# Weights fetched two groups ahead instead of three, and loads for row sums issued half an interval sooner

## The chip, the cores and the metric

The kernel is one program on one core of a Trainium2 chip. The metric is device time in microseconds (us) of one execution; lower is better. The engines are named as the profile names them: PE (TensorE, the matrix products), DVE (VectorE), ACT (ScalarE), POOL (GpSimd) and SP (SyncE, which here only issues DMAs). Each engine works through its own instructions in a fixed order, and waits on semaphores for what others write.

## What is computed

One layer of a hybrid encoder: 512 positions, width 2048, one batch entry. Cut to what matters:

```python
mod = jax.nn.silu(c) @ w_cond[layer] + b_cond[layer]
shift, scale, gate = jnp.split(mod, 3, axis=-1)
h = rms_norm(x) * (1.0 + scale[:, None]) + shift[:, None]
proj = h @ w_in[layer]
aq, ak, av, ag, gq, gk, gv, gg, lr_f, lr_b = jnp.split(proj, PROJ_SPLITS, axis=-1)
...  # A) 16 heads of dilated window attention over aq, ak, av, three patterns merged by their softmax sums
a_out = att.reshape(B, S, ATT_WIDTH) * jax.nn.silu(ag)
...  # B) gated linear attention, 4 heads, forward and backward scan, chunks of 64
g_o = rms_norm(o_fwd + o_bwd).reshape(B, S, GLA_WIDTH) * gla_norm_gain[layer]
g_out = g_o * jax.nn.silu(gg)
y = jnp.concatenate([a_out, g_out], axis=-1) @ w_out[layer]
x = x + gate[:, None] * y
return rms_norm(x) * final_gain
```

All is float32. `shift`, `scale` and `gate` depend on `c` alone; so does what `shift` adds to the projections.

## The kernel before, in words

**Stages.** First the condition row and the normalised input are made. Then come the units of the input projection, one after the other on PE: qk2, qk4, qk6 (queries and keys of the attention heads), gk, gv0, gv1 (keys and values of the linear attention), ag0, ag1 (attention gates), gg0, gg1 (linear attention gates), and then the output projection. A unit (`unit`, L1014) computes a block of 512 columns in four PSUM tiles. Its weights come in eight groups of 128x1024 floats. For each group, ACT rounds the raw tile to a high half (`split_hi`, L433, written at L444; for example `gk2h`), DVE subtracts it to get the low half (`split_lo`, L425, written at L430; `gk2l`), and PE makes three products (`three`, L216 to L219): high by high, low by high, high by low.

**Side work.** Between the products of a unit stand other jobs, at positions from 0 to 1 within the unit: attention scores, turns and values in qk2 to gk (`attention`, L712; a score's p at L736, its RECIPROCAL at L740, POOL's scaling at L744, PE's turn into t at L756, and the pieces pt at L760 and L761), the heads of the linear attention in gv1 to gg0 (`gla_head`, L865), and what the change is about, the row sums. In the linear attention, `norm` takes the sum of two squares (gsq, L978 and L981), splits it into gsh (ACT, L988) and gsl (DVE, L989), and PE adds them up over partitions into gn (L990, L991).

**The row sums.** 48 pieces of weights, 128x1024 floats or 512 KB each, are multiplied by a row and summed along the row on DVE: 16 for the bias that `shift` adds (`bias_half`: load L845, sum at L850 for the first half and L316 for the second, tile rawv), and 32 for `gate` (`gate_half`: load L809, sum L316, tile rawg). A name such as v20 or g121 gives the number m and the half z: rawv20 is m = 2, z = 0; rawg121 is m = 12, z = 1. Each has a load and a sum as two jobs of the unit; `some_sums` (L859) gives both their positions, and `SUMS_IN` says how many fall to each unit (4 to qk6, 4 to gk, 9 to gv0, 3 to gv1, 7 to ag0, 8 to ag1, 9 to gg0, the rest to gg1).

**Tiles.** Raw weights and many sum pieces share one pool of four tiles (`RAW`, L247, `bufs=4`). The other sum pieces use two single tiles, "h" and "l": all second halves of the bias, and the odd gate pieces for m below 12 or z = 1. A load waits on SP until its tile is free, and all loads behind it on SP wait with it.

**What sets the order.** PE's order is written out by hand. For DVE, ACT, POOL and SP a scheduler orders the instructions when the program is built, by the order of the code, and jobs of the side list are given some preference (`urgent`, L1008). So when a load moves in the code, its sum can move in DVE's order as well.

**POOL's transfers.** Sums of output weights are formed in DRAM by software DMAs that POOL issues (`paced`, L390; tile T, L393). Each waits until ACT has made a certain high half of a weight.

Of the kernel before, what the change touches and what calls it, by code (L numbers as in the profile page):

```python
# [114 lines left out]
SUMS_IN = {"qk6": 4, "gk": 4, "gv0": 9, "gv1": 3, "ag0": 7, "ag1": 8, "gg0": 9}  # L115
# [63 lines left out]
def block_kernel(ctx: ExitStack, tc: tile.TileContext, a: dict):  # L179
# [21 lines left out]
    def PJ(name):  # L201
        return pp.tile([P, 512], F32, tag="pj", bufs=5, name=name)
# [151 lines left out]
    def fetch(i):  # L354
        if i < len(groups) and i not in raws:
            u, g = groups[i]
            if u == "O":
                raws[i] = out_fetch(g)
            else:
                raws[i] = RAW(f"raw_{u}{g}", [2, 512])  # L360
                nc.sync.dma_start(raws[i], a["w_" + u][g])
# [54 lines left out]
    def block_sums(name):  # L416
        n = SUM_OPS_IN[name]
        r = [sum_ops.pop(0) for _ in range(n)]
        return [((q + 0.5) / n, x) for q, x in enumerate(r)]
# [202 lines left out]
    n = len(chain) // 2  # L622
# [4 lines left out]
    for z in range(2):  # L627
        for e in range(3):
            name = ("mm", "a", 0, 7) if (z, e) == (1, 2) else ("m0", z, e)
# [229 lines left out]
    def some_sums(name):  # L859
        r = [sum_work.pop(0) for _ in range(SUMS_IN.get(name, len(sum_work)))]  # L860
        n = len(r)
        loads = [(max(q - 0.3, 0.1) / n, x[0]) for q, x in enumerate(r)]
        return sorted(loads + [((q + 0.7) / n, x[1]) for q, x in enumerate(r)], key=lambda x: x[0])

    def gla_head(h):  # L865
# [142 lines left out]
    def urgent(go):  # L1008
        with tc.high_priority(offset=20):
            go()  # L1010
# [3 lines left out]
    def unit(name, natural, side=(), lr=None):  # L1014
        side = sorted(spill + list(side) + block_sums(name), key=lambda x: x[0])
        spill[:] = [(at - 1, go) for at, go in side if at >= 1]
        side = [x for x in side if x[0] < 1]
        ps = [PJ(f"ps_{name}_{i}") for i in range(4)]
        pos, tick, ticks = 0, 0, 64
        for g in range(KT // 2):  # L1020
            i0 = gi[name, g]
            split_hi(i0)
            split_hi(i0 + 1)
            for ahead in (2, 3):
                fetch(i0 + ahead)
            split_lo(i0)
            hi, lo = wts[i0]
            for i in range(4):
                for kk in range(2):
                    k = 2 * g + kk  # L1030
                    rh, rl = h_hi[:, k, :], h_lo[:, k, :]
                    if natural:
                        t = slice(i * P, i * P + P)
                        cw = slice(kk * 512, kk * 512 + 512)
                        three(ps[i], rh[:, t], rl[:, t], hi[:, cw], lo[:, cw], k == 0, k == KT - 1)
                    else:
                        c = slice(kk * 512 + i * P, kk * 512 + i * P + P)
                        three(ps[i], hi[:, c], lo[:, c], rh, rl, k == 0, k == KT - 1)
                    tick += 1
                    if tick % 8 == 2:  # L1040
                        split_lo(i0 + 1)
                    while pos < len(side) and side[pos][0] * ticks <= tick:
                        urgent(side[pos][1])
                        pos += 1
                if lr is not None:
                    lr(4 * g + i)
        while pos < len(side):
            urgent(side[pos][1])
            pos += 1
        return ps  # L1050
# [396 lines left out]
```

## Time and profile before

| what | value |
| --- | --- |
| time, median of 3 runs | 948.0 us (945.02 to 949.52) |
| profiled execution | 947.69 us, span 945.9 us |
| mean granted TensorE clock | 0.991 |
| PE busy | 920.1 us, 97% of the span |
| DVE, ACT, POOL busy | 69%, 50%, 10% |
| DVE's waits for rawg loads | 43.8 us in 19 waits |
| SP's waits for a tile of rawg, a gate sum to end (L809) | 41.1 us in 14 waits |
| rawg load, issue to landing, median | 5.3 us |
| POOL's transfer T<-in_w_o, issue to landing, median | 5.2 us |

Rows of a timeline begin with the start and the duration in us; a duration holds the engine's pipeline, so rows of one engine overlap a little at their ends. `[3.49 <-DVE st L736]` at the end says that the engine had been idle for 3.49 us before this row, until DVE wrote st at L736. A list of waits has the total in us, the number, and the longest.

### The profile page before, as it was taken

To read this page: it belongs to the slowest core of one execution; us is meant where nothing else is said; L and a number is where in the kernel's file an instruction comes from. 1 tells how busy PE (TensorE), PEld (TensorE's weight loads), DVE (VectorE), ACT (ScalarE), POOL (GpSimd) and SP (SyncE) were. 2 spreads that over 40 slices of the span, in tenths; PEclk is the share of its full clock that TensorE was granted. 3 is DMA by queue.
4 is the path that set the end of the run, shared out by engine and by line. 5 is a ranking of instruction groups with operands and counts; after the bars stand their busy time and mean duration, and the time that the engine had idled before them with its cause. 6 is when DMAs were issued, how large, how long until landed. Compare 5 with 4: busy or idle time off the path is not lost.

```text
span 945.9 us, 12130 instructions
## 1 busy us (share of the span) xinstructions
PE 920.1 (97%) x4375; PEld 761.9 (81%) x4375; DVE 655.3 (69%) x960; ACT 471.9 (50%) x770; POOL 98.6 (10%) x152
## 2 busy tenths in 40 slices
PE   8999999999999989999999999999999999999996
PEld 6888888888888878788877888878777888888884
DVE  7988899775756666766544656585686629697496
ACT  5553543565655545555413545363553428555464
POOL 0000000022222132122000100111001000000001
PEclk9999999999999989999999999999999999999998
DMA  9999496656656764745766646776766566956753
GB/s 350 404 411 375 183 372 245 223 176 165 191 190 161 220 212 132 236 165 142 212 211 188 185 156 198 223 222 209 248 195 183 184 170 250 324 201 217 276 179 133
DMA packets 54629, 210.84 MB, mean 223 GB/s; under 512 B 7237, under 2 KB 7525, under 8 KB 46249
## 3 DMA queue, kind: packets, MB, share of 16 engines
q1 hardware_dynamic: 48946, 175.89, 51.3%
q0 software_dynamic: 5184, 33.62, 15.0%
q8 instruction: 34, 0.56, 0.2%
q10 hardware_dynamic: 440, 0.57, 0.2%
q14 instruction: 25, 0.20, 0.1%
HBM read 201.57 MB, written 37.84 MB: 253 GB/s over the span
## 4 chain that ended last, share of the span: by engine, by line
PE 78%; DMA 8%; DVE 7%; issue 3%; ACT 2%; POOL 0%; SPq 0%; DVEq 0%; POOLq 0%; ACTq 0%
DMA rawg<-in_wg 5%; PE ps_qk L217 4%; PE ps_qk L218 4%; PE ps_qk L219 4%; PE g L219 4%; PE g L217 4%; PE g L218 4%; PE stb L219 3%; PE ps_gv L219 3%; PE ps_gv L218 3%; PE ps_gv L217 3%; PE stb L218 3%; PE stb L217 3%; PE o L770 3%; PE sta L218 2%
## 5 line engine op out<-in xcount | busy, mean ns | idle before, releaser
L739 ACT ACTIVATE p<-p,st 128x512 f32<-128x512 f32 x64 | 46.1, 720 | 59.7 <-DVE st L736 58.9
L316 DVE CUSTOM_DVE_ANT_0 cb<-cb,sb,c_bcond 128x2048 f32<-128x2048 f32 (+1 forms) x32 | 73.5, 2295 | 0.8 <-DMA cb<-in_wm 0.8
L393 POOL DMA_DIRECT2D T<-in_w_o x48 | 33.5, 705 | 317.7 <-ACT qk21h L444 119.8
L744 POOL TENSOR_SCALAR p<-p,st 128x512 f32<-128x512 f32 x62 | 45.0, 726 | 201.3 <-DVE st L740 153.1
L761 DVE TENSOR_TENSOR pt<-t,pt 128x512 fp32r<-128x512 f32 x64 | 43.8, 688 | 16.3 <-ACT pt L760 16.0
L736 DVE CUSTOM_DVE_ANT_0 p<-s,g 128x512 f32<-128x512 f32 x64 | 43.7, 687 | 14.2 <-PE s L733 14.0
L756 PE MATMUL t<-c_ident,p 128*128 128x128 f32 x256 | 39.1, 275 | 5.2 <-DVE st L736 3.5
L756 PEld LDWEIGHTS t<-c_ident,p 128*128 128x128 f32 x256 | 31.5, 141 | 15.6 <-issue 4.2
L760 ACT ACTIVATE pt<-t 128x512 fp32r<-128x512 f32 x64 | 37.9, 591 | 10.6 <-PE t L756 9.5
L770 PEld LDWEIGHTS o<-pt,vv 128*128 128x128 f32 x256 | 35.5, 193 | 3.0
L770 PE MATMUL o<-pt,vv 128*128 128x256 f32 x256 | 36.2, 285 | 0.0
L316 DVE CUSTOM_DVE_ANT_0 rawg<-rawg,crow,gate 128x1024 f32<-128x1024 f32 x16 | 20.4, 1282 | 22.5 <-DMA rawg<-in_wg 22.5
L316 DVE CUSTOM_DVE_ANT_0 rawg<-rawg,crow,c_bcond 128x1024 f32<-128x1024 f32 x16 | 20.4, 1282 | 21.2 <-DMA rawg<-in_wg 21.2
L740 DVE RECIPROCAL st<-st 128x1 f32<-128x1 f32 x64 | 10.3, 161 | 23.7 <-ACT p L739 23.7
L732 PE MATMUL s<-ks,qs 128*128 128x512 f32 x64 | 25.1, 392 | 0.0
L733 PE MATMUL s<-kl,qs 128*128 128x512 f32 x64 | 25.0, 390 | 0.0
L944 ACT ACTIVATE sq<-st,sc 128x256 f32<-128x256 f32 x24 | 12.2, 506 | 21.2 <-DVE st L934 13.4
L850 DVE CUSTOM_DVE_ANT_0 rawv<-rawv,shb 128x1024 f32<-128x1024 f32 x8 | 10.0, 1250 | 16.4 <-DMA rawv<-in_wv 16.4
L777 DVE TENSOR_TENSOR cat<-o,oh 64x256 f32<-64x256 f32 x32 | 13.3, 415 | 11.0 <-ACT oh L773 10.7
L773 ACT ACTIVATE oh<-o 64x256 f32<-64x256 f32 x32 | 12.2, 382 | 16.9 <-PE o L770 16.0
L1272 POOL TENSOR_SCALAR x<-x,rn 128x512 f32<-128x512 f32 x3 | 3.4, 1144 | 158.3 <-ACT rn L1261 158.3
L508 ACT ACTIVATE h_hi<-xt,shift 128x512 fp32r<-128x512 f32 x16 | 11.5, 719 | 13.0 <-DVE shift L316 13.0
(1520 smaller groups left out, 2977.7 us busy)
## 6 DMA issues: line engine op xcount, KB each, us to landing
cb<-in_wm SPq DMA_DIRECT2D x31, 1024.0 KB, 8.8
T<-in_w_o POOLq DMA_DIRECT2D x48, 512.0 KB, 5.2
rawg<-in_wg SPq DMA_DIRECT2D x32, 512.0 KB, 5.3
raw_O<-T SPq DMA_DIRECT2D x32, 512.0 KB, 4.8
raw_qk<-in_w_qk SPq DMA_DIRECT2D x24, 512.0 KB, 3.6
raw_O<-in_w_o SPq DMA_DIRECT2D x24, 512.0 KB, 4.1
rawb<-in_w_sb SPq DMA_DIRECT2D x16, 512.0 KB, 5.7
rawv<-in_wv SPq DMA_DIRECT2D x16, 512.0 KB, 4.4
```

What stands on the lines that cost most here:

```text
L217: mm(ps, lh, rh, start=first, stop=False, skip_group_check=more)
L218: mm(ps, ll, rh, start=False, stop=False, skip_group_check=more)
L219: mm(ps, lh, rl, start=False, stop=last, skip_group_check=more)
L316: nc.vector.tensor_tensor_reduce(out=w, in0=w, in1=with_, op0=ALU.mult, op1=ALU.add, scale=1.0, scalar=init, accum_out=dst)
L393: move = nc.gpsimd.dma_start(dst, src, max_dma_last_dim=8192, **how).ins
L736: nc.vector.tensor_tensor_reduce(out=t, in0=ps, in1=gt[h][:, P * i:P * i + 512], op0=ALU.add, op1=ALU.min, scale=1.0, scalar=3e38, accum_o ...
L739: act(t, t, AF.Exp, bias=st[:, 0:1], scale=-1.0, accum_out=st[:, 1:2])
L744: last["pool"] = nc.gpsimd.tensor_scalar(t, t, st[:, 2:3], 1.0, op0=ALU.mult, op1=ALU.mult).ins
L756: nc.tensor.transpose(pk[:, kt * P:kt * P + P], t[:, kt * P:kt * P + P], ident)
L760: act(hi, src, AF.Copy)
L761: tt(lo, src, hi.bitcast(F32), op=ALU.subtract)
L770: mm(po[:, :256], vv[h // 4][:, kt, h % 4, :], t[:, w, kt, :], start=kt == 0 and w == 0, stop=kt == 3 and w == 1)
```

## The change

Two expressions change.

```diff
     def some_sums(name):
         r = [sum_work.pop(0) for _ in range(SUMS_IN.get(name, len(sum_work)))]
         n = len(r)
-        loads = [(max(q - 0.3, 0.1) / n, x[0]) for q, x in enumerate(r)]
+        loads = [(max(q - 0.8, 0.05) / n, x[0]) for q, x in enumerate(r)]
         return sorted(loads + [((q + 0.7) / n, x[1]) for q, x in enumerate(r)], key=lambda x: x[0])
...
             i0 = gi[name, g]
             split_hi(i0)
             split_hi(i0 + 1)
-            for ahead in (2, 3):
+            for ahead in (2,) if name in SUMS_IN or name == "gg1" else (2, 3):
                 fetch(i0 + ahead)
             split_lo(i0)
```

The load of the q-th sum of a unit stands at (q - 0.8)/n instead of (q - 0.3)/n of the unit, and the first at 0.05/n instead of 0.1/n; the sums stay at (q + 0.7)/n. In the units that carry sums, a weight group is fetched when the group two before it is begun, and not three before. qk2, qk4 and the output projection keep both. The pool of four raw tiles is as before; no tile is added.

The number of instructions stays the same on every engine, PE's and POOL's orders stay as they were, and SP's and DVE's change. At the start of gk, DVE's order had these rows (rawv20 and rawv21 are the two halves of bias sum 2; p, st and t carry head and position block, so p112 is head 11, block 2):

```order
L740 RECIPROCAL st111_3353<-st111_3353 128x1
L761 TENSOR_TENSOR pt101_3317<-t103_3362,pt101_3317 128x4x128
L736 ISA p112_3378,st112_3379<-s112_3375,g11_3201 128x512
L736 ISA st112_3379 128x1
L850 ISA rawv20_3558,vbias0_1495<-rawv20_3558,shb_2894 128x1024
L850 ISA vbias0_1495 128x1
L740 RECIPROCAL st112_3379<-st112_3379 128x1
L316 ISA rawv21_3618,vbias_1494<-rawv21_3618,shb_2894,vbias0_1495 128x1024
L316 ISA vbias_1494 128x1
L761 TENSOR_TENSOR pt110_3387<-t110_3388,pt110_3387 128x4x128
L777 TENSOR_TENSOR cat1_2918<-o101_3398,oh101_3407 64x256
```

Now they stand further up, next to blocks 0 and 1 of the same head:

```order
L736 ISA st103_3281 128x1
L740 RECIPROCAL st103_3281<-st103_3281 128x1
L850 ISA rawv20_3552,vbias0_1495<-rawv20_3552,shb_2894 128x1024
L850 ISA vbias0_1495 128x1
L761 TENSOR_TENSOR pt100_3242<-t101_3290,pt100_3242 128x4x128
L736 ISA p110_3303,st110_3304<-s110_3300,g11_3201 128x512
L736 ISA st110_3304 128x1
L316 ISA rawv21_3564,vbias_1494<-rawv21_3564,shb_2894,vbias0_1495 128x1024
L316 ISA vbias_1494 128x1
L761 TENSOR_TENSOR pt101_3315<-t102_3316,pt101_3315 128x4x128
L740 RECIPROCAL st110_3304<-st110_3304 128x1
L430 TENSOR_TENSOR gk0l_3424<-raw_gk0_3342,gk0h_3423 128x1024
```

Both halves of the sum have moved up past the scores p111 and p112 and the low half of gk0 (it stands between the two places), the first half past p110 too.

At the start of gg1, DVE had these rows around the norm of head 3 (gsq31, gsl3; S3l is the low half of an operand of the output projection):

```order
L316 ISA rawg111_6197,gate_1492<-rawg111_6197,crow1_5485,gate0_1493 128x1024
L316 ISA gate_1492 128x1
L1151 TENSOR_TENSOR S3l_6263<-diff0_6367,S3h_6262 128x1024
L981 TENSOR_TENSOR gsq31_6175<-gsq31_6175,gsq30_6162 128x512
L316 ISA rawg121_6280,gate_1492<-rawg121_6280,crow1_5485,gate0_1493 128x1024
L316 ISA gate_1492 128x1
L989 TENSOR_TENSOR gsl3_6213<-gsq31_6175,gsh3_6212 128x512
L316 ISA rawg131_6322,gate_1492<-rawg131_6322,crow1_5485,gate0_1493 128x1024
L316 ISA gate_1492 128x1
L1151 TENSOR_TENSOR S3l_6263<-diff1_6407,S3h_6262 128x1024
```

And now:

```order
L316 ISA rawg111_6186,gate_1492<-rawg111_6186,crow1_5471,gate0_1493 128x1024
L316 ISA gate_1492 128x1
L316 ISA rawg121_6274,gate_1492<-rawg121_6274,crow1_5471,gate0_1493 128x1024
L316 ISA gate_1492 128x1
L1151 TENSOR_TENSOR S3l_6261<-diff0_6367,S3h_6260 128x1024
L981 TENSOR_TENSOR gsq31_6173<-gsq31_6173,gsq30_6160 128x512
L1151 TENSOR_TENSOR S3l_6261<-diff1_6405,S3h_6260 128x1024
L989 TENSOR_TENSOR gsl3_6211<-gsq31_6173,gsh3_6210 128x512
L316 ISA rawg131_6286,gate_1492<-rawg131_6286,crow1_5471,gate0_1493 128x1024
L316 ISA gate_1492 128x1
```

g121 has moved ahead of S3l and gsq31, and the second S3l ahead of gsl3; g131 stays behind gsl3.

On SP the loads that belong to it stood in this order:

```order
L809 DMA rawg111_6197<-in_wg 128x1024
L361 DMA raw_gg13_6271<-in_w_gg1 128x1024
L809 DMA rawg121_6280<-in_wg 128x1024
L809 DMA rawg131_6322<-in_wg 128x1024
L361 DMA raw_gg14_6307<-in_w_gg1 128x1024
L809 DMA rawg151_6462<-in_wg 128x1024
```

And now:

```order
L809 DMA rawg111_6186<-in_wg 128x1024
L809 DMA rawg121_6274<-in_wg 128x1024
L361 DMA raw_gg13_6307<-in_w_gg1 128x1024
L809 DMA rawg131_6286<-in_wg 128x1024
L361 DMA raw_gg14_6340<-in_w_gg1 128x1024
L809 DMA rawg151_6429<-in_wg 128x1024
```

The load of g121 has passed that of weight group 3 of gg1. The same exchange of a weight and a sum load, with a sum moving ahead of gsq on DVE, is found in ag1 (g120 past ag13) and in gg0 (g41 past gg03). In gg0, g61 moves up to stand right behind g51, g81 takes its old place, and the old place of g81, between qi31 (L906) and gg05l, is empty.

## The prediction

> **What bounds the kernel now.** I read the busy times first, then what TensorE (PE) waited for, then the rows of PE that begin after a gap, then the granted clock behind the larger gaps.
>
> ```profile
> PE 920.1 (97%) x4375; PEld 761.9 (81%) x4375; DVE 655.3 (69%) x960; ACT 471.9 (50%) x770; POOL 98.6 (10%) x152
> ```
>
> ```profile
> PE gn L991 <- DVE gsl L989: 5.4, 3, 2.1
> PE t L756 <- DVE st L736: 3.5, 1, 3.5
> ```
>
> PE is the bound: it is busy for 97% of the span, and no other engine comes near. The change touches no matrix product, so it can win only what PE now waits for, and lose only by new waits. The waits list says how little that is: three waits of the GLA norm for its low half (gsl) make 5.4 us, and one wait for a score makes 3.5. These are the gaps in the stretch that the change touches, each in the brackets at the end of its row:
>
> ```profile
> 349.37 1.08 PE L756 MATMUL t<-c_ident,p 128*128 128x128 f32 x4 [3.49 <-DVE st L736]
> ...
> 386.45 0.63 PE L756 MATMUL t<-c_ident,p 128*128 128x128 f32 x4 [0.81 <-DVE pt L761]
> ...
> 389.36 0.66 PE L756 MATMUL t<-c_ident,p 128*128 128x128 f32 x4 [0.44 <-POOL p L744]
> ...
> 618.78 0.50 PE L991 MATMUL gn<-gsl,ones 128*128 128x512 f32 x1 [1.83 <-DVE gsl L989]
> ...
> 674.63 0.50 PE L991 MATMUL gn<-gsl,ones 128*128 128x512 f32 x1 [1.44 <-DVE gsl L989]
> ...
> 709.43 0.70 PE L927 MATMUL kv<-gv,kit 128*128 128x256 f32 x2 [0.80 <-DVE st L939]
> ...
> 733.09 0.51 PE L991 MATMUL gn<-gsl,ones 128*128 128x512 f32 x1 [2.13 <-DVE gsl L989]
> ```
>
> They add up to 10.9 us. A gap can cost more than its length, since the clock may fall behind it. The columns are the stretch, its length, each engine's busy time, and then the granted clock:
>
> ```profile
> 618.80:622.20 3.40, 3.40 (x15) 2.78 (x16) 2.47 (x3) 2.81 (x4) 0.00 (x0) 1.00 0.95 351
> ...
> 733.80:737.20 3.40, 3.40 (x10) 2.62 (x9) 3.40 (x6) 3.03 (x4) 0.00 (x0) 0.50 0.92 369
> ```
>
> After the 1.83 us gap the clock stayed at 1.00, after the 2.13 us gap it was 0.50 for 3.4 us, in which PE did half of 3.4 us of work: 1.7 us lost.
>
> **The change part by part.** Every instruction is kept; loads and sums only change places, on SP's queue and on VectorE's (DVE).
>
> *Fetching two groups ahead.* A weight load now goes out behind the sum load that takes its place. The shortest lead I find is that of group 5 of qk6, whose load moves from 323 to the place of the next one, 329.29:
>
> ```profile
> 329.29 0.34 SPq L361 DMA_DIRECT2D raw_qk<-in_w_qk  x1
> ...
> raw_qk<-in_w_qk SPq DMA_DIRECT2D x1, 512.0 KB, 5.3
> ...
> 342.49 1.06 ACT L444 ACTIVATE qk65h<-raw_qk 128x1024 fp32r<-128x1024 f32 x1 [0.95 <-PE ps_qk L219]
> ```
>
> It lands at 334.6 and ScalarE (ACT) first reads it at 342.49: 7.9 us to spare. A load would have to take 13 us before this hurts. Cost 0; the cover is this lead, and without it each further microsecond would be one of PE.
>
> *The 349 gap.* In qk6 VectorE's order is unchanged. What holds it up is the second half of bias sum 1, a z=1 half, which uses the single tile "h" that the sum before frees:
>
> ```profile
> 339.26 7.93 DMA rawv<-in_wv
> ...
> 347.32 1.28 DVE L316 CUSTOM_DVE_ANT_0 rawv<-rawv,shb,vbias 128x1024 f32<-128x1024 f32 x1 [5.08 <-DMA rawv<-in_wv]
> ```
>
> That load stands in the same place of SP's queue and waits for the same tile, so "sooner" does nothing for it; a weight load stands where the other sum load stood ahead of it, with as many bytes. I leave the gap and its clock loss as they are: 0.
>
> *The start of gk.* Here bias sum 2 (v20, then v21) moves from 383 to 372, between score rows:
>
> ```profile
> 372.20 0.16 DVE L740 RECIPROCAL st<-st 128x1 f32<-128x1 f32 x1 [0.88 <-ACT p L739]
> ...
> 372.82 0.69 DVE L761 TENSOR_TENSOR pt<-t,pt 128x512 fp32r<-128x512 f32 x1 [0.46 <-ACT pt L760]
> ...
> 375.00 0.16 DVE L740 RECIPROCAL st<-st 128x1 f32<-128x1 f32 x1 [0.88 <-ACT p L739]
> ...
> 377.58 0.68 DVE L736 CUSTOM_DVE_ANT_0 p<-s,g 128x512 f32<-128x512 f32 x1
> ...
> 383.14 1.22 DVE L850 CUSTOM_DVE_ANT_0 rawv<-rawv,shb 128x1024 f32<-128x1024 f32 x1 [1.95 <-DMA rawv<-in_wv]
> ...
> 377.90 0.60 PE L756 MATMUL t<-c_ident,p 128*128 128x128 f32 x4
> ...
> L744 POOL TENSOR_SCALAR p<-p,st 128x512 f32<-128x512 f32 x62 | 45.0, 726 | 201.3 <-DVE st L740 153.1
> ...
> 368.93 0.33 SPq L361 DMA_DIRECT2D raw_gk<-in_w_gk  x1
> ...
> raw_gk<-in_w_gk SPq DMA_DIRECT2D x1, 512.0 KB, 3.1
> ```
>
> The load of v20 takes the place of a gk weight, issued at 368.93 and landed 3.1 us later, so it is there at about 372.1. v20 then runs from 372.4 to 373.6, pt and the next score (0.7 each) to 375.0, v21 (1.28) to 376.3, pt to 377.0 and the RECIPROCAL of 375.00 to 377.1. GpSimd's scaling takes 0.73 and PE turns that score at 377.90: just in time. The idle times of VectorE in brackets (0.46, 0.88) swallow most of the insertion. So there is no new gap, and 1.95 us of wait with both sums leave 383 to 386, which removes the gaps at 386.45 and 389.36: **-1.25**. The other end: if the load takes 5.3 us as the qk row above, v20 is 1.9 us later, a gap of 1.9 appears, and the net is +0.65. I take -1.25, since the 3.1 row is the load at that very place.
>
> *The start of gv0* repeats this: bias sum 4 moves up by 10 us, and bias sum 5 takes its old place:
>
> ```profile
> 449.94 1.23 DVE L850 CUSTOM_DVE_ANT_0 rawv<-rawv,shb 128x1024 f32<-128x1024 f32 x1 [1.00 <-DMA rawv<-in_wv]
> ```
>
> The insertion costs 0 (up to +1.9, as above), and since another sum stands in the old place with such a wait, nothing is gained: **0**.
>
> *The three norm gaps.* In gg1 SP issued a weight (gg13) at 721.40 and sum load g121 at 722.56, and a GpSimd software transfer started beside them, at 721.57. Their times to landing, in this order:
>
> ```profile
> 721.40 0.33 SPq L361 DMA_DIRECT2D raw_gg<-in_w_gg  x1
> 722.56 0.33 SPq L809 DMA_DIRECT2D rawg<-in_wg  x1
> ...
> raw_gg<-in_w_gg SPq DMA_DIRECT2D x1, 512.0 KB, 7.3
> ...
> rawg<-in_wg SPq DMA_DIRECT2D x1, 512.0 KB, 8.4
> ...
> T<-in_w_o POOLq DMA_DIRECT2D x1, 512.0 KB, 8.8
> ```
>
> All three are twice as slow as the lone load of 3.1. The change swaps the two SP rows: g121 lands where gg13 did, at 728.7 instead of 731.0; gg13 lands at 731.0 and is read at 745.46, so that costs nothing. But VectorE's order moves with it:
>
> ```profile
> 725.09 1.23 DVE L1151 TENSOR_TENSOR S3l<-diff,S3h 128x1024 fp32r<-128x1024 f32 x1
> 726.23 0.68 DVE L981 TENSOR_TENSOR gsq<-gsq,gsq 128x512 f32<-128x512 f32 x1
> ...
> 731.14 1.28 DVE L316 CUSTOM_DVE_ANT_0 rawg<-rawg,crow,gate 128x1024 f32<-128x1024 f32 x1 [4.23 <-DMA rawg<-in_wg]
> 732.35 0.69 DVE L989 TENSOR_TENSOR gsl<-gsq,gsh 128x512 fp32r<-128x512 f32 x1
> ...
> 726.95 0.63 ACT L988 ACTIVATE gsh<-gsq 128x512 fp32r<-128x512 f32 x1 [1.04 <-DVE gsq L981]
> ...
> 745.46 1.06 ACT L444 ACTIVATE gg13h<-raw_gg 128x1024 fp32r<-128x1024 f32 x1 [2.47 <-PE ps_gg L219]
> ```
>
> Now S3l, gsq, ACT's gsh and a second S3l were done ahead of or during the wait; after the change all stand behind g121. By start to start from the rows: g121 at 728.9, S3l at 730.1, gsq at 731.2, second S3l at 731.8 (gsh beside it), gsl at 733.0 instead of 732.35. PE goes on 0.6 later: **+0.6**. Ends: if the software transfer starts behind g121, it lands in 3.1 us and the gap with its clock loss goes (-3.8); if g121 lands at 731.0 all the same, +2.9 and a second slow stretch of 1.7 (+4.6). I take the swap, since two loads in one queue are what the rows show.
>
> [...]
>
> In ag1 and gg0 the same swap gives the sum load 1.2 (the distance of the two issues) to 2.3 us (gg1's gain), and only gsq and gsh come behind it, 0.6 and 0.7: a net between +0.1 and -1.0 at each. I take **0** at both, as the gain by issue order is what is certain.
>
> *The rest of gg0.*
>
> ```profile
> 681.34 1.28 DVE L316 CUSTOM_DVE_ANT_0 rawg<-rawg,crow,gate 128x1024 f32<-128x1024 f32 x1 [3.10 <-DMA rawg<-in_wg]
> ...
> 703.12 1.29 DVE L316 CUSTOM_DVE_ANT_0 rawg<-rawg,crow,gate 128x1024 f32<-128x1024 f32 x1 [0.78 <-DMA rawg<-in_wg]
> ```
>
> One sum moves from 692.9 to 676, ahead of a 3.10 us idle time that covers its 1.28 (with 1.8 us left for its own load; beyond that each microsecond may reach PE). The next takes its place, and nothing stands at 703 any more: 2.1 us of VectorE's time ahead of the states (st) that PE misses at 709.43. **-0.8** (0 at worst).
>
> The sums that move in gv0, gv1 and ag0 stand where no gap of PE is, before or behind: 0.
>
> Sum: -1.25 + 0 + 0.6 + 0 - 0.8 = -1.45 us. The profiled run took 947.7 us, so 946.2; the median of the runs, 948.0, is 0.3 above it: **946.5**. Less than 0.5% (4.7 us) can't be told from no change by a measurement of this kernel.
>
> **The rivals.**
> *Sum loads come clear of the software transfers.* The loads go out sooner in the order, so they might land ahead of the transfer, and VectorE would not wait in front of gsl. Against it: the loads wait for a free tile, not for their turn, and the transfers keep their places. It would take away 1.83 + 1.44 + 2.13 and 1.7 of clock, and the 0.6 I add: 946.5 - 7.7 = 938.8.
>
> *A late sum holds up the scores (slower).* At 372 or 440 the sum stands between scores that PE needs within about a microsecond. It decides from a load of about 3.5 us upwards, and the 8.4 of g121 shows what a load beside a software transfer takes. With 8.4 at gk's start v20 comes 4.9 us late: a gap as long, and a slow stretch or two (1.7 to 3.4, say 2.5): 946.5 + 4.9 + 2.5 = 953.9, and at both places 961. For it: 349 shows just this, a wait of 5.08 on VectorE and 3.49 on PE. Against it: the gk weight at that place took 3.1. [...]
>
> *gg1 waits longer.* g121 lands at 731.0 with all the rest behind it: 946.5 - 0.6 + 4.6 = 950.5.
>
> *Weights come late.* Two groups ahead leave too little lead where loads take 8 us or more. Against it the 7.9 us of the shortest lead; it would give a gap or two of 2 us with clock: about 953.
>
> *It does little of what it says.* The code has no fifth raw tile: the pool keeps four, and z=1 loads wait for their single tile, so most sums just change places: 948.
>
> **How the numbers follow.** My forecast 0.42; clear of transfers 0.14; late sum 0.18; gg1 longer 0.12; weights late 0.06; little changes 0.08. Within 0.5% (943.3 to 952.7) fall the forecast, gg1, "little" and none of the others: 0.62; faster 0.14; slower 0.24. Without gg1's ends, which are rivals of their own, the bounds of the terms add to -3.45 (1.25, 1.0, 1.0 and 0.8, less 0.6) and +3.35 (0.65, 1.9, twice 0.1, and 0.6), so about the median of 948.0 the likeliest case alone has 944.5 to 951.4. The range reaches to part of the late-sum case and leaves out the faster one and the tail of the slower: 942 to 954.
>
> **What would show it.** Right: the 349 gap is there unchanged; no gap at 386; gaps at 618, 674 and 733 end on gsl within a microsecond of now, with gsl behind gsq directly after a rawg sum; no gap at kv near 709; clock 0.50 after 733 alone in the second half. Wrong: a gap at a score's turn (L756) near 376 or 444 behind a waiting rawv; gn gaps of none or of over 3 us; PE waiting for a low half of weights (L430).

## The result and the profile after

| | before | after |
|---|---|---|
| median of the runs | 946.64 us (944.12 to 949.52, 11 runs) | 940.5 us (937.76 to 944.03, 11 runs) |
| ratio of the medians, 95% interval | | 0.9938 (0.9922 to 0.9955) |
| profiled execution | 947.7 us, span 945.9 | 941.06 us, span 939.3 |

The change makes the kernel 0.6% faster. That is more than the 0.5% bound and 1.5 us below the range of the forecast. A second measurement, with other runs of the kernel before beside it, is told below as "after, again" and gave 0.9916.

The page of the kernel after begins with the busy times:

```profile
PE 916.8 (98%) x4375; PEld 759.5 (81%) x4375; DVE 655.9 (70%) x960; ACT 471.7 (50%) x770; POOL 99.4 (11%) x152
```

PE has the same instructions and 3.3 us less busy time, since fewer of its products ran at half clock: between 300 and 760 us the clock was 0.50 for 10.2 us in the profile before (348.05 to 354.88 and 733.76 to 737.18) and for 3.4 in the profile after (349.75 to 353.15). The list of PE's waits (in total, times, the longest), with only the entries on scores, on the norm and on gates:

```profile
PE t L756 <- DVE st L736: 3.8, 1, 3.8
...
PE t L756 <- ACT p L742: 1.3, 1, 1.3
PE gn L990 <- ACT gsh L988: 1.2, 2, 1.0
PE kt L915 <- DVE ki L905: 0.9, 1, 0.9
...
PE gn L991 <- DVE gsl L989: 0.4, 2, 0.2
```

The wait for gsl has gone from 5.4 us to 0.4. The norm now waits 1.2 for its high half (gsh), which it did not before, and two waits are longer: one on a score (ACT p, 1.3 for 0.5) and one on a gate operand (ki, 0.9 for 0.7). PE's rows behind these gaps, in order of time:

```profile
349.79 0.45 PE L756 MATMUL t<-c_ident,p 128*128 128x128 f32 x1 [3.77 <-DVE st L736]
...
455.32 0.44 PE L756 MATMUL t<-c_ident,p 128*128 128x128 f32 x2 [1.33 <-ACT p L742]
...
617.00 0.51 PE L990 MATMUL gn<-gsh,ones 128*128 128x512 f32 x1 [0.98 <-ACT gsh L988]
...
617.73 0.50 PE L991 MATMUL gn<-gsl,ones 128*128 128x512 f32 x1 [0.22 <-DVE gsl L989]
...
700.30 0.44 PE L915 MATMUL kt<-c_ident,ki 128*128 128x128 f32 x2 [0.91 <-DVE ki L905]
```

Nothing stands here for gk's start (386, 389), for the states near 709 or for the norm near 733. The clock behind the first of them and behind the norm of gg1, with the columns of the prediction (the granted clock is the last number but two):

```profile
349.75:353.15 3.40, 3.36 (x10) 2.90 (x11) 3.06 (x7) 2.04 (x5) 2.07 (x2) 0.50 0.43 163
...
727.30:730.70 3.40, 3.40 (x16) 2.81 (x15) 1.15 (x1) 3.08 (x4) 0.53 (x1) 1.00 0.69 271
```

The half clock behind 349 is still there; that behind the third norm is gone.

**Where the 6.6 us came from.** All the kernels below run the same products in the same order, so PE's first product (L217) with a given weight group is a milestone. This table holds the time between milestones, worked out from PE's rows, for one profiled execution of each kernel (qk64 is weight group 4 of qk6). Only stages in which something moved are shown.

| | profiled us | qk63 to qk64 (349) | qk64 to gk0 (gk's start) | gk0 to gv00 (gv0's start) | ag06 to ag10 (norm 617) | ag10 to ag16 (kt near 640) | ag16 to gg00 (norm 674) | gg00 to gg04 (kt near 700) | gg04 to gg10 (kv 709, norm 733) |
|---|---|---|---|---|---|---|---|---|---|
| before | 947.7 | 15.38 | 36.13 | 66.84 | 17.99 | 38.25 | 17.56 | 25.12 | 34.94 |
| after | 941.1 | 14.72 | 34.72 | 67.93 | 17.59 | 38.25 | 16.81 | 25.45 | 29.84 |
| after less before | -6.6 | -0.66 | -1.41 | +1.09 | -0.40 | 0 | -0.75 | +0.33 | **-5.10** |
| before_p2 | 950.7 | 15.79 | 36.23 | 67.31 | 17.81 | 38.25 | 17.72 | 25.46 | 36.60 |
| before_p3 | 947.0 | 14.09 | 35.98 | 67.04 | 17.74 | 38.23 | 17.65 | 25.13 | 35.35 |
| after, again | 937.4 | 14.33 | 34.74 | 67.29 | 15.84 | 38.79 | 15.84 | 25.65 | 29.86 |
| e1 | 947.3 | 16.62 | 35.92 | 67.25 | 17.83 | 38.25 | 17.19 | 27.85 | 30.80 |
| e2 | 940.3 | 14.27 | 34.73 | 66.59 | 15.84 | 39.32 | 15.84 | 28.30 | 29.84 |
| e5 | 942.5 | 15.33 | 36.19 | 67.10 | 15.84 | 42.93 | 15.84 | 24.23 | 30.10 |
| e6 | 937.7 | 14.56 | 34.75 | 67.11 | 15.84 | 39.18 | 15.84 | 24.23 | 29.86 |
| e8 | 941.0 | 14.13 | 34.73 | 67.12 | 15.84 | 40.45 | 15.84 | 25.79 | 32.24 |
| e9 | 944.9 | 15.61 | 35.65 | 67.46 | 17.80 | 38.25 | 17.53 | 25.16 | 31.66 |
| e9, again | 943.6 | 15.36 | 36.14 | 67.13 | 17.11 | 38.25 | 17.43 | 25.12 | 31.22 |
| e10 | 948.1 | 15.93 | 36.38 | 66.97 | 18.07 | 38.25 | 17.81 | 25.85 | 31.53 |
| e11 | 947.8 | 13.91 | 34.72 | 68.00 | 15.84 | 39.33 | 16.60 | 28.54 | 36.21 |
| e3 | 934.9 | 9.18 | 34.75 | 67.25 | 15.84 | 39.08 | 16.55 | 26.13 | 29.86 |

Most of it is the last stage, from the middle of gg0 to the start of gg1, for which I had forecast -0.2 (+0.6 at the norm, -0.8 at the states).

What happened there is told by the issues. SP's and GpSimd's rows of the kernel after, at the start of gg1:

```profile
716.63 1.54 SPq L809 DMA_DIRECT2D rawg<-in_wg  x2
...
718.97 0.79 POOL L393 DMA_DIRECT2D T<-in_w_o  x1 [8.23 <-ACT gg10h L444]
...
719.97 0.33 SPq L361 DMA_DIRECT2D raw_gg<-in_w_gg  x1
```

The two rawg are g111 and g121, the second issued at 717.84. The list of transfers, with the time from issue to landing last, has for g111, g121, T and gg13:

```profile
rawg<-in_wg SPq DMA_DIRECT2D x1, 512.0 KB, 3.2
...
rawg<-in_wg SPq DMA_DIRECT2D x1, 512.0 KB, 4.4
...
T<-in_w_o POOLq DMA_DIRECT2D x1, 512.0 KB, 8.7
...
raw_gg<-in_w_gg SPq DMA_DIRECT2D x1, 512.0 KB, 8.3
```

Before, g121 was issued 0.99 us behind T and took 8.4. Now it is issued 1.13 ahead of T and takes 4.4; the weight group, which nobody needs soon, is the one that takes 8.3. VectorE therefore comes through early:

```profile
722.34 1.28 DVE L316 CUSTOM_DVE_ANT_0 rawg<-rawg,crow,gate 128x1024 f32<-128x1024 f32 x1 [1.14 <-DMA rawg<-in_wg]
723.55 1.22 DVE L1151 TENSOR_TENSOR S3l<-diff,S3h 128x1024 fp32r<-128x1024 f32 x1
724.69 0.69 DVE L981 TENSOR_TENSOR gsq<-gsq,gsq 128x512 f32<-128x512 f32 x1
...
726.43 0.69 DVE L989 TENSOR_TENSOR gsl<-gsq,gsh 128x512 fp32r<-128x512 f32 x1
```

The order is the forecast one (sum, S3l, gsq, second S3l, gsl), but the wait in front of the sum is 1.14 us where it was 4.23.

What held g121 in its old place is told by the waits of SP and GpSimd in the kernel before, and by VectorE's row between them:

```profile
721.57 0.79 POOL L393 DMA_DIRECT2D T<-in_w_o  x1 [7.26 <-ACT gg10h L444]
...
721.30 1.23 DVE L430 TENSOR_TENSOR gg10l<-raw_gg,gg10h 128x1024 fp32r<-128x1024 f32 x1
...
SPq L809 <- DVE gg10l L430: 0.7, 1, 0.7
```

T waits for the high half gg10h, and g121 for the tile that VectorE frees with the low half gg10l, one step later. So in all five profiles in which g121 stands behind gg13 (before, before_p2, before_p3, e1, e10) it is issued 0.99 behind T. The swap gives it a tile that a gate sum frees, and its place no longer hangs on gg10h.

Of the 2.12 us by which g121 moved against T, the swap gives 1.16 (the distance of the two issues of before, 721.40 and 722.56). The rest, 0.96, I put down to the other term of my own sum: nothing stands on VectorE at 703 any more, so it comes sooner to the sums g91 and g101, which free the raw tiles for which the loads of g111 and g121 wait. That is the explanation which the experiments test: *the place of g121 against T decides, and it takes both the swap and the empty place at 703 to bring it ahead.* The rival explanations were that one half of the change does it all, that T costs nothing and VectorE's order alone decides, and that one profile of before was just an unlucky one.

### The profile page after: what moved, and what is told of

It reads as the page before. It is cut to its first block, busy times and chain, and to the rows that moved or that the text cites. A ratio compares the mean times of both kernels' runs of the same rounds, so it can differ in the third digit from the quotient of the medians.

```text
span 939.3 us, 12130 instructions
## 1 busy us (share of the span) xinstructions
PE 916.8 (98%) x4375; PEld 759.5 (81%) x4375; DVE 655.9 (70%) x960; ACT 471.7 (50%) x770; POOL 99.4 (11%) x152
## 4 chain that ended last, share of the span: by engine, by line
PE 83%; DVE 7%; DMA 6%; issue 2%; ACT 2%; ACTq 0%; DVEq 0%
PE ps_qk L218 4%; PE ps_qk L217 4%; PE ps_qk L219 4%; PE g L219 4%; PE g L217 4%; PE g L218 4%; PE stb L219 3%; PE stb L218 3%; PE stb L217 3%; PE o L770 3%; PE ps_gv L219 3%; PE ps_gv L218 3%; PE ps_gv L217 3%; PE t L756 3%; DMA rawg<-in_wg 3%; PE sta L218 2%
```

## The experiments

Each ratio is to the kernel before, measured beside it, with its 95% interval. All of these kernels compute the whole reference; e8 alone does more, two multiplications whose result nobody reads.

### e1 and e2: each half of the change alone

e1 has the load positions only, e2 the fetching two ahead only.

```diff
 e1
-        loads = [(max(q - 0.3, 0.1) / n, x[0]) for q, x in enumerate(r)]
+        loads = [(max(q - 0.8, 0.05) / n, x[0]) for q, x in enumerate(r)]
 e2
-            for ahead in (2, 3):
+            for ahead in (2,) if name in SUMS_IN or name == "gg1" else (2, 3):
```

> Only the sum loads are placed half an interval sooner; weights are still fetched three groups ahead. The built order shows that in gg1 the load of g121 stays behind that of weight gg13 and that the gk start is as before, but that in gg0 no sum stands at 703 any more. Lead theory (a load lands in 3 to 4.4 us when it is issued 1.1 us or more ahead of POOL's transfer, in 7 to 8.5 when issued less than about 0.2 us ahead or behind it; and what gave gg1 its 4 us is that DVE got 1 us earlier there and g121 went ahead of gg13): the gap at kv near 709 goes (-0.8), VectorE is about 1 us earlier at gg1, but g121 is issued right at the transfer and still takes about 7 us; the gap near 733 stays at 1 to 2 us. In all 1 to 3 us faster than before. Rival (the sooner loads by themselves clear the transfers): the gaps near 618, 674 and 733 all go, 6 us or more.

> Only the fetch is changed, to two groups ahead; the loads keep their old positions. The built order shows the same exchange of g121 and gg13 as the whole change, the same places of bias sum 2 at the start of gk, and no sum at 703. Lead theory: nearly the whole gain, no gap near 386 and 733, 5 to 7 us faster than before. Rival (the gain is that of the sooner loads): within 2 us of before.

e1: 948.1 us, 1.0037 (1.0012 to 1.0063). e2: 944.26 us, 0.997 (0.9954 to 0.9987); its profiled execution, 940.3, was its fastest. The waits of e1, then those of e2:

```profile
PE gn L991 <- DVE gsl L989: 3.4, 3, 1.7
PE kt L915 <- DVE ki L905: 3.2, 2, 2.6
```

```profile
PE kt L915 <- DVE ki L905: 4.5, 3, 2.7
...
PE gn L991 <- DVE gsl L989: 0.5, 1, 0.5
```

e2 swaps weight and sum load at all three norms and takes the norm gaps away (15.84 in both ag stages, 29.84 in the last). e1 leaves the weights ahead and keeps three norm waits of up to 1.7. But both pay near 700. There VectorE has a sum and the low halves gg04l and gg05l between one gate operand ki and the next, and PE waits up to 2.7 us (27.85 and 28.30 where the kernel before has 25.12); with both edits the sum stands ahead of the first ki and gg05l behind the second, and the wait is 0.91 (25.45). So neither half is the whole, and the halves are not additive: e1 costs 0.4%, e2 gains 0.3%, both gain 0.6 to 0.8%. Why e1 is slower and not just equal isn't settled: its last stage is faster by 4.1, that near 700 slower by 2.7, and the 349 stage was 1.2 longer in this one profile.

### e5 and e9: the kernel before, with the software transfer moved

`block_sums` sets at which place in a unit GpSimd's transfers are issued. e5 moves the last one of ag0, ag1 and gg0 by 0.1 of a unit, so that it comes into the next unit; e9 does so in gg0 alone. Neither has anything of the change.

```diff
-        return [((q + 0.5) / n, x) for q, x in enumerate(r)]
+        return [((q + 0.5) / n + (0.1 if name in ("ag0", "ag1", "gg0") and q == n - 1 else 0), x) for q, x in enumerate(r)]
```

> The kernel before, with three of POOL's transfers (the last of ag0, ag1 and gg0, those at 607.6, 664.0 and 721.6) moved past the end of their unit, so that each waits for the next high half of a weight, some 9 us later. The orders of SP and VectorE are those of before. Lead theory: the loads g120, g41 and g121 then land in 3 to 4.5 us instead of 7.3 to 8.4, the three norm gaps go with the clock loss behind 733: 6 to 7 us faster than before without any part of the change. Rival (the three waits come from the place of the loads in SP's queue or from the weights' bytes): gaps of 1.4 to 2.1 stay, no change within 1 us.

> The kernel before, with only the last of POOL's transfers of gg0 (the one at 721.6) moved behind the next high half. Lead theory: the load of g121 lands in about 4.4 us, the gap of 2.13 near 733 and the slow stretch behind it go, and nothing behind the last head's norm waits for VectorE, so the gain is kept: 3.5 to 4.5 us faster than before, with the gaps near 618 and 674 as they were. Rival (what PE gains there is given back at the next wait on VectorE): under 1 us.

> The kernel before with the one transfer of gg0 moved, again. If the loss near 733 is in every execution of the kernel before: 2.5 to 4.5 us faster in the median. If it is there in some: 0 to 2 us faster, and a smaller spread than the kernel before.

e5: 942.86 us, 0.9966 (0.9948 to 0.9985). All three norm gaps are gone (15.84, 15.84, 30.10), without the change, and the three sum loads take 5.2, 4.7 and 4.4 us where they took 8.0, 7.3 and 8.4. So it is T that makes the sum loads slow, and VectorE's order alone is no explanation. But of the 8.7 us that these three stages gain in its profile the median gains only 3.6, for in ag1 PE comes sooner to a gate operand that VectorE has not finished. PE's row, and the clock behind it:

```profile
645.81 0.55 PE L915 MATMUL kt<-c_ident,ki 128*128 128x128 f32 x3 [2.83 <-DVE ki L905]
```

```profile
646.50:649.90 3.40, 3.40 (x10) 2.67 (x9) 1.96 (x3) 1.28 (x3) 0.81 (x2) 0.50 0.97 376
```

2.83 of gap and a slow stretch give 4.7 us back (42.93 for 38.25).

e9: 944.79 us, 0.9991 (0.9971 to 1.001), and again 944.26 us, 0.9976 (0.9957 to 0.9995). Its last stage is 31.66 and 31.22, so 3.3 to 3.7 shorter than that of the profile of before. The norm gap at 733 is gone, and what is left to the 29.84 of after is the wait of PE for the states, which e9 does not touch:

```profile
710.76 0.70 PE L927 MATMUL kv<-gv,kit 128*128 128x256 f32 x2 [1.54 <-DVE st L939]
```

By their ratios the runs gain less than the stage, 0.9 and 2.3 us.

### before_p2 and before_p3: the kernel before, profiled twice more

> The kernel before once more, for a second profile, since moving the transfer in gg1 alone took away 4 us near 733 in the profile and yet hardly moved the median. If the gap of 2.13 with its slow stretch is in every execution: gaps on gsl near 618, 674 and 733 of about 1.8, 1.4 and 2.1 and a slow stretch after 733. If it came by chance in the first profile: a gap under 1 us or no slow stretch near 733, and a span 2 to 4 us shorter.

> As the run before it, a third profile of the kernel before: the same two expectations.

945.62 us, 0.9982 (0.9958 to 1.0007), and 946.5 us, 0.9997 (0.9971 to 1.0022): the same kernel, as it must be. But the profiles differ from the first one in the stage that matters. Rows of VectorE and PE, the landing of that sum's load and the clock, of the first of the two:

```profile
706.34 1.28 DVE L316 CUSTOM_DVE_ANT_0 rawg<-rawg,crow,gate 128x1024 f32<-128x1024 f32 x1 [2.62 <-DMA rawg<-in_wg]
...
712.66 0.70 PE L927 MATMUL kv<-gv,kit 128*128 128x256 f32 x2 [2.67 <-DVE st L939]
...
737.67 0.50 PE L991 MATMUL gn<-gsl,ones 128*128 128x512 f32 x1 [1.87 <-DVE gsl L989]
```

```profile
rawg<-in_wg SPq DMA_DIRECT2D x1, 512.0 KB, 7.2
```

```profile
713.50:716.90 3.40, 3.40 (x10) 2.63 (x9) 2.28 (x4) 1.50 (x3) 1.25 (x2) 0.50 0.38 53
```

and of the second:

```profile
710.18 0.70 PE L927 MATMUL kv<-gv,kit 128*128 128x256 f32 x2 [2.60 <-DVE st L939]
...
734.05 0.50 PE L991 MATMUL gn<-gsl,ones 128*128 128x512 f32 x1 [0.71 <-DVE gsl L989]
```

The sum that stands at 703 in the first profile (g81) waited 0.78 us there for a load that took 5.4; here the load took 7.2 and VectorE waited 2.6. PE then loses 2.6 to 2.7 and a slow stretch at the states near 710, and less at the norm, which was 2.13 with a slow stretch in the first profile and is 1.87 and 0.71 here. Where the stage loses thus changes from execution to execution; how much it loses does so less: 34.94, 36.60, 35.35. In after it is 29.84 and 29.86. The gain of 5.1 to 6.7 is no accident of one profile, and the sum at 703 is the larger cause in two profiles of three. In these two the place in front of g121's, where gg13 stood, was already 1.66 and 1.68 ahead of T, with the sum still at 703. So the 0.96 above is measured against the first profile alone.

### after, again, and e6: after with the transfers moved too

e6 is the kernel after with e5's line.

> The changed kernel once more, for a second profile of it and a comparison on the same chip as the others. Lead theory: 5 to 7 us faster than before; no gap above 0.7 near 727 and no slow stretch behind it. The gaps near 617 and 672 and at kt near 640 may come out otherwise than in the first profile, since profiles of kernels with the same orders there have differed: where the norm gap near 617 is gone, a gap on ki near 642 is expected in its place. Rival (the 4 us at the last norm were chance of one execution): a gap of about 2 us near 727 with a slow stretch.

> The changed kernel with the last transfers of ag0, ag1 and gg0 moved behind the next high half. Lead theory: near 727 nothing changes, as the loads are clear of the transfer there already; the norm gaps near 617 and 672 go (1.2 and 0.4), and at most that is gained; a gap on ki near 642 gives it back: from 1.5 us faster to 3 us slower than the changed kernel. Rival (the transfers still cost the changed kernel as much as they cost the kernel before): 5 us faster than the changed kernel.

After, again: 939.1 us (936.44 to 940.62), 0.9916 (0.9893 to 0.9939). e6: 938.83 us, 0.9911 (0.9887 to 0.9935). With the sum loads ahead of the transfers, moving the transfers adds nothing that can be measured: e6's last stage is the same 29.86. The two edits take the same wait away.

### e8: after with VectorE made late

Two multiplications of 128x512 on VectorE behind `at` of head 3, ahead of the sums that free the tiles for g111 and g121.

```diff
+            if h == 3:
+                late = T2("late")
+                for _ in range(2):
+                    masked.append(tt(late, at, at, op=ALU.mult).ins)
```

> The changed kernel with two idle multiplications of 128x512 on VectorE (0.6 us each) between the masked product of head 3 and the next gate sum, so that g91, g101 and with them the loads of g111 and g121 come 1.2 us later, and the place in the queues is kept. Lead theory: g121 is issued within 0.2 us of POOL's transfer and takes 7 us or more instead of 4.4; a gap of 2 to 3 us on gsl comes back near 730, and with it a stretch at half clock: 4 to 5 us slower than the changed kernel. Rival (the exchange with gg13 in SP's queue is enough): no gap near 730, at most 0.5 us slower than the changed kernel.

942.96 us, 0.9961 (0.9942 to 0.9981): part of the gain is gone. The swap is still there; VectorE is 1.4 later, and one S3l has stepped back behind gsq, which shortens the way to the norm. SP's row with g111 and g121 (the second at 716.89, T at 716.60), g121's landing, and PE's rows:

```profile
715.68 1.53 SPq L809 DMA_DIRECT2D rawg<-in_wg  x2
```

```profile
rawg<-in_wg SPq DMA_DIRECT2D x1, 512.0 KB, 7.4
```

```profile
727.03 0.51 PE L994 MATMUL gn<-gsh,ones 128*128 128x512 f32 x1 [1.28 <-ACT gsh L992]
...
728.11 0.50 PE L995 MATMUL gn<-gsl,ones 128*128 128x512 f32 x1 [0.57 <-DVE gsl L993]
```

g121 went from 1.13 ahead of T to 0.29 behind it, its time from 4.4 to 7.4, and the norm gap is back (1.28 and 0.57; lines 992 to 995 are 988 to 991 of the others), but without a slow stretch. The stage is 32.24, 2.4 longer than in after, and the ratio is 0.9961 where after has 0.9938 and 0.9916, which is 2.2 to 4.3 us. Not all of that need be g121: near 640 this profile is 1.7 to 2.2 longer too. For the last stage this is the closest test of the explanation. With the order of SP and of the sums as after has it, g121 lands 4.4 later against T, 1.4 by its later issue and 3.0 by its longer time, and the norm waits again.

### e10 and e11: the change in gg0 alone, and everywhere but in gg0

e10 empties the place at 703, but leaves gg13 ahead of g121 in gg1; e11 has the swap in gg1, but leaves the sum at 703.

```diff
 e10
+        loads = [((max(q - 0.8, 0.05) if name == "gg0" else max(q - 0.3, 0.1)) / n, x[0]) for q, x in enumerate(r)]
+            for ahead in (2,) if name == "gg0" else (2, 3):
 e11
+        loads = [((max(q - 0.3, 0.1) if name == "gg0" else max(q - 0.8, 0.05)) / n, x[0]) for q, x in enumerate(r)]
+            for ahead in (2,) if (name in SUMS_IN and name != "gg0") or name == "gg1" else (2, 3):
```

> Both edits in gg0 alone; all other units as before. In the built order no sum stands ahead of the states near 703, g41 is exchanged with gg03 and stands ahead of gsq; in gg1 g121 stays behind gg13. Place theory (the sum that left the place near 703 is what gave most): no gap at kv near 709 and no slow stretch there; PE needs 30 to 31.5 us from its first product with group 4 of gg0 to its first with group 0 of gg1, against 35 to 36.6 in three profiles of the kernel before and 29.9 in two of the changed kernel; near 733 at most 1 us of gap is left, since VectorE comes about 2 us earlier to the loads of g111 and gg13. In all 3.5 to 5.5 us faster than before. Rival (the exchange of g121 and gg13 in gg1 is needed): 33 us or more for that stretch, under 2 us faster than before.

> Both edits in all units but gg0; gg0 as before, with its sum near 703, and in gg1 g121 ahead of gg13 as in the changed kernel. Place theory: a gap of 0.8 to 2.7 at kv near 709; g121 is issued about as early against POOL's transfer as gg13 was and takes 5 to 8 us; 34 to 37 us for the stretch of PE from group 4 of gg0 to group 0 of gg1; from the rest of the change 1.4 at the start of gk and about 1 net in ag1: 1.5 to 4 us faster than before. Rival (the exchange in gg1 suffices): under 32 us for that stretch, 5 us or more faster than before.

e10: 945.03 us, 0.9979 (0.9958 to 1.0). e11: 946.88 us, 0.9999 (0.9976 to 1.0021). PE's row at the norm in e10:

```profile
735.15 0.51 PE L991 MATMUL gn<-gsl,ones 128*128 128x512 f32 x1 [1.42 <-DVE gsl L989]
```

and PE's rows in e11, with g121's landing (issued at 720.18, T at 720.33):

```profile
693.30 0.62 PE L915 MATMUL kt<-c_ident,ki 128*128 128x128 f32 x3 [2.45 <-DVE ki L905]
...
732.17 0.49 PE L990 MATMUL gn<-gsh,ones 128*128 128x512 f32 x1 [2.67 <-ACT gsh L988]
...
733.24 0.50 PE L991 MATMUL gn<-gsl,ones 128*128 128x512 f32 x1 [0.58 <-DVE gsl L989]
```

```profile
rawg<-in_wg SPq DMA_DIRECT2D x1, 512.0 KB, 8.1
```

The last stage can be split in two. PE's time from its first product with gg04 to that with gg05 holds the states, that from gg07 to gg10 the norm; in between nothing moves by more than 0.1. Worked out from PE's rows:

| | swap | sum at 703 | gg04 to gg05 (states) | gg07 to gg10 (norm) |
|---|---|---|---|---|
| before, before_p2, before_p3 | no | yes | 7.85, 11.30, 11.21 | 9.93, 8.11, 6.91 |
| after, again; e2 | yes | no | 6.76, 6.78; 6.76 | 5.92, 5.92; 5.92 |
| e1; e10 | no | no | 6.78; 6.76 | 6.86; 7.61 |
| e11 | yes | yes | 7.72 | 11.33 |
| e9, e9 again (T moved) | no | yes | 8.58, 8.14 | 5.92, 5.92 |
| e8 (VectorE late) | yes | no | 6.78 | 8.30 |

The empty place takes away the loss at the states, with the swap or without it. At the norm it leaves 0.9 (e1) and 1.7 (e10), with g121 still 0.99 behind T and taking 7.0 and 7.7; the swap takes that away. So against the first profile the empty place alone gives 3.4 and 4.1 of the 5.1. The swap alone (e11) brings g121 to 0.15 ahead of T, where gg13 stood before (0.17 ahead), and that is not enough: it takes 8.1, S3l and gsq stand behind it as I had forecast, and the stage is 36.21. In this execution both edits are needed, as the explanation says; whether the swap alone would do in one like before_p2 or before_p3, no run shows.

What does not fit is the totals: -0.2% and 0.0% don't add up to the -0.6 to -0.8% of both. In e11 a part of it is seen, since without gg0's share of the change the time won at the ag norms is lost near 693 (28.54 in that stage, with 2.45 of gap and half clock behind it). In e10's profile the stage of ag0 (ag00 to ag06) is 2.06 longer than in any other kernel. VectorE's rows there, of e10 and of the kernel before:

```profile
576.63 1.28 DVE L316 CUSTOM_DVE_ANT_0 rawg<-rawg,crow,c_bcond 128x1024 f32<-128x1024 f32 x1 [8.92 <-DMA rawg<-in_wg]
```

```profile
571.81 1.28 DVE L316 CUSTOM_DVE_ANT_0 rawg<-rawg,crow,c_bcond 128x1024 f32<-128x1024 f32 x1 [4.93 <-DMA rawg<-in_wg]
```

This load took 10.1 us in e10 and 6.1 in before, and PE then waited 0.35 and 0.89 for VectorE. Whether that is there in most of e10's runs is open; the profiled one, 948.1, is among its two slowest.

Taken together, e1, e2, e5, e9, e10 and e11 all gained less in the median than their expectations by the explanation. The explanation holds for the last stage; what the stages gain is not kept in full, and only part of why has been found.

### e3: after, with the cause of the 349 gap taken away

The second half of bias sum 1 waits for the tile "h" of the sum before. e3 puts it into the tile "l".

```diff
-            t.append(two.tile([P, 1024], F32, tag="h", name=f"rawv{m}{z}") if z else RAW(f"rawv{m}{z}", [1024]))
+            t.append(two.tile([P, 1024], F32, tag="l" if m == 1 else "h", name=f"rawv{m}{z}") if z else RAW(f"rawv{m}{z}", [1024]))
```

> The changed kernel with the second half of bias sum 1 (rawv11) in the single tile l instead of h, so that its load doesn't wait for the sum before it. Lead theory: the wait of 5 us on VectorE at 347 and PE's gap of 3.5 to 4.6 near 350 go, with one or two slow stretches of 1.7 us each: 5 to 7 us faster than the changed kernel, so 11 to 13 faster than before. Rival (the transfer of POOL at 337 makes another load late and the gap only moves): under 2 us faster than the changed kernel.

933.87 us (931.46 to 935.21), 0.9858 (0.9832 to 0.9883): 5.2 us faster than after beside it, and the fastest kernel of the study. Its waits:

```profile
PE kt L915 <- DVE ki L905: 2.1, 3, 0.9
...
PE t L756 <- ACT p L742: 0.9, 1, 0.9
```

The wait of 3.8 for a score is gone, and with it the slow stretch: that stage is 9.18 us where after has 14.3 to 14.7. So the prediction named the cause of the 349 gap rightly (the single tile), and this is a loss that the change left in place.

## Why the prediction was right in part and wrong in the sum

**Right: the start of gk.** Forecast -1.25, measured -1.41 in the profile after, and between -1.38 and -1.41 in every other kernel with that swap. Both halves of bias sum 2 run without a wait:

```profile
371.85 1.23 DVE L850 CUSTOM_DVE_ANT_0 rawv<-rawv,shb 128x1024 f32<-128x1024 f32 x1
...
374.21 1.28 DVE L316 CUSTOM_DVE_ANT_0 rawv<-rawv,shb,vbias 128x1024 f32<-128x1024 f32 x1
```

**Right: the weights.** No wait of PE for a weight group appears, so two groups ahead cost 0.

**Right: the 349 gap stays, by its own cause.** 3.77 for 3.49. The stage's -0.66 is one slow stretch where the first profile of before had two; before_p3 has one as well and 14.09. Kernels with both edits there have 13.9 to 14.7, those with neither 14.1 to 15.9; I have not found whether that is more than chance.

**A size off: the start of gv0.** Forecast 0 (up to +1.9), measured +1.09. The other kernels with the whole change have +0.3 to +0.5 against the first profile of before, and e11, which has the change there too, +1.16. But the other two profiles of before have +0.2 and +0.5 as well, so only part of it is sure. In the profile of after the sum there waits longer:

```profile
449.15 1.23 DVE L850 CUSTOM_DVE_ANT_0 rawv<-rawv,shb 128x1024 f32<-128x1024 f32 x1 [2.16 <-DMA rawv<-in_wv]
```

I said that bias sum 5 stands in the old place with "such a wait". But the scores run 1.9 us sooner by what the stages ahead have won, and the load is issued only 1.0 sooner, so the wait grew from 1.00 to 2.16 and a gap of 1.33 at 455 came of it.

**The step that failed: "The three norm gaps".** I priced the swap in gg1 at +0.6, with "g121 lands where gg13 did". From gg07 to gg10, where this norm stands, the change gave -4.0 in the first pair of profiles, and -2.2 and -1.0 against the other two of before. With the swap and the empty place g121 lands 4.4 to 5.0 after its issue (after, after again, e2, e3), not the 7.3 of gg13. I had written down the case that came, -3.8 "if the software transfer starts behind g121", and set it aside since "two loads in one queue are what the rows show". They are, but the third row of that same fence, T's, was the one that mattered, and the place that g121 was to take was not fixed against T: gg13 stood 0.17, 1.66 and 1.68 ahead of it in three profiles of the same kernel. (The three transfers of that fence, 7.3 to 8.8 us, were 2.4 to 2.8 times as slow as the lone 3.1, and not twice.) My next term, nothing at 703 any more, moves VectorE by about 1 us against T in the first pair, and VectorE frees the tiles for these loads. I took that gain at the states only (-0.8, measured -1.1) and did not carry it on to the next loads. Against the rival "sum loads come clear of the software transfers" I wrote that "the loads wait for a free tile, not for their turn": true, and just the reason why a faster VectorE brings them forward, once the swap has given g121 a tile that does not hang on gg10h. That rival's 938.8 is nearest to what was measured (940.5, 939.1).

The two smaller norms were forecast at 0 and gave -0.4 and -0.8 in the first profile, -2.1 and -1.7 in the second. There the sum load is issued 0.4 to 0.6 ahead of T where it was 1.0 to 1.6 behind. What they win is partly handed back at the next gate operand (ki), up to 4.7 in e5.

**The second failing, of size: "The rest of gg0", with one profile taken as typical.** The loss at the states was 0.80 in the profile I read and 2.6 to 2.7 with half clock behind it in the next two. From gg04 to gg05 the change therefore gave -1.1 against the first profile, but -4.5 and -4.4 against the others, for a forecast of -0.8. So between the two terms the larger miss is the norm in the first profile and the states in the other two. Had I seen those two profiles, the term of gg0 would have been -2.6 (the gap) to -4.3 (with 1.7 of clock) in place of -0.8, and the sum -3.3 to -5.0, some 943 to 945, even with the norms as I had them. In the one profile, the row that could have warned is the 0.78 us of wait in front of the sum at 703: a load that is just late in one execution may be later in others.

**The rivals.** "A late sum holds up the scores" came only in small: where the sums moved in between scores, at 372 and 438, none waits, but at 449 the wait of 2.16 brought the gap of 1.33 at a score, where the rival asked for 4.9. "gg1 waits longer" came in e11 only. "Weights come late" and "it does little" fell.

For the slow stretches I followed the rows (half clock behind the gap of 2.13, none behind 1.83). That gaps of this size can be followed by half clock held: 2.60 and 2.67 at the states and 2.83 in e5 were. But a gap's length alone does not decide it, since 2.6 in e1 and 2.7 in e2, near 700, were not; the last section has the numbers.

## What to carry to other kernels

When a step leaves an engine, follow that engine on to the next tile it frees and to the load that waits for that tile: in e8 1.4 us more on VectorE put a load behind another engine's transfer instead of ahead of it, and the stage took 2.4 longer. Ask also what the load's tile hangs on: in its old place g121 could not come ahead of T, since one weight's halves released both. Before a wait on a load is priced from one profile, look how near the load is to another queue's transfer; near that edge its time is not one number (g81's load took 5.4 us in one execution of the kernel before and 7.2 in two others), and another profile of the same kernel is worth more than another row of the first. And a gap taken away upstream is a gain only as far as the next engine in the chain can follow: in e5 the gate operand took more than half of it back.

## What the runs showed of the hardware

**A load's time went with where the other queue's transfer stood.** The shortest 512 KB loads of SP named here took 3.1 us (a gk weight in before) and 3.2 (g111 in after). In gg1, g121 took 4.4 to 5.0 when it was issued 1.13 to 1.65 ahead of GpSimd's transfer (after, after again, e2, e3), 8.1 and 7.4 at 0.15 ahead and 0.29 behind (e11, e8), and 7.0 to 8.4 at 0.99 behind (five profiles). At other places the same lead gave other times: the sum loads at the two ag norms, 0.4 to 0.6 ahead, took 5.2 to 7.8; in ag1 two loads 0.20 ahead of a transfer took 3.8 and 3.7 (after, e6) and one 0.12 behind it 3.5 (after again); g81's in gg0, 1.0 behind, took 5.4 in one execution of before and 7.2 in two others. So for g121 a lead of 1.13 or more went with 4.4 to 5.0 us, and 0.15 or less, or a place behind, with 7.0 to 8.4, but over all places the lead does not fix the time. g121's 7.4 and 8.1 are more than twice the 3.1 to 3.2. A further load of SP was under way beside it and the transfer, and how much each of the two adds no run here separates.

**The clock fell behind some gaps of PE and not behind others of the same length.** It was 0.50 behind 2.13 us near 733 (before), 2.60 and 2.67 at the states (before_p3 and before_p2), 2.83 near 646 (e5), 3.49 near 349 (before) and 3.77 there (after). In e11 the products behind 2.45 near 693 took 0.63 us where they take 0.39 to 0.40 at clock 1.00. It stayed at 1.00 behind 1.83 (before, 618.80 to 622.20). Behind 2.6 in e1 and 2.7 in e2, near 700, the stages leave no room for half clock: they are 2.73 and 3.18 longer than that of before, little more than the gaps, where a gap with the 1.7 us of a slow stretch would give 4.3 and 4.4. The clock behind the 2.60 of before_p3:

```profile
711.70:715.00 3.30, 3.30 (x9) 2.55 (x8) 2.06 (x3) 1.33 (x3) 1.70 (x3) 0.50 0.53 79
```

The 349 gap cost one slow stretch or two: half clock lasted 6.8 us there in before and 3.4 in after. What decides between gaps of the same length no run here separates.
